# Seven block products for three down projections of the first feed-forward, with partial sums and the residual stream in HBM, and a tail without GpSimd

## The chip, the cores and the metric

The kernel runs on one core of a Trainium2 chip. A core has five engines that work beside each other: TensorE (PE, matrix products; PEld is its weight loading), VectorE (DVE), ScalarE (ACT), GpSimd (POOL) and SyncE (SP, which here only starts DMAs). Each executes its own list of instructions in order and waits on semaphores. The metric is the device time of one launch in microseconds. Before the change the median is 879.47 us of three runs, from 879.43 to 879.74. All data are fp32.

## The reference, cut to what matters

One layer of a decoder on x of 512 tokens by 1024 channels: a half-step feed-forward, a mixer, a second half-step feed-forward, each with an RMS norm ahead of it and another behind it.

```
def swiglu(x, w_gu, w_down):
    gate, up = jnp.split(x @ w_gu, 2, axis=-1)
    return (jax.nn.silu(gate) * up) @ w_down
...
x = x + 0.5 * rms_norm(swiglu(rms_norm(x, ffn1_pre_g[l]), ffn1_w_gu[l], ffn1_w_down[l]), ffn1_post_g[l])
y = hybrid_mixer(rms_norm(x, mix_pre_g[l]), ...)
x = x + rms_norm(y, mix_post_g[l])
x = x + 0.5 * rms_norm(swiglu(rms_norm(x, ffn2_pre_g[l]), ffn2_w_gu[l], ffn2_w_down[l]), ffn2_post_g[l])
```

The hidden width is 2816, which is 22 chunks of 128. `w_gu` is 1024 by 5632 and `w_down` 2816 by 1024. The change concerns the down product (the last `@ w_down`) of the first feed-forward and the last norm, the last line, for the last 128 tokens.

## The kernel before, in words

*Precision.* An fp32 product is made of three products of rounded halves: a weight or an activation is split into a high part (a cast on ACT) and a low part (a subtraction on DVE), and PE computes hi·hi, hi·lo and lo·hi (`mm3`, L403 to L408).

*Weights.* The class `Weights` (L50) streams all weights through five raw buffers of 1 MB (`NRAW`). A raw buffer holds several units; for each unit, `cast` makes the high part and `low` the low part. `take` hands the next unit to PE and first makes the units up to four ahead (`AHEAD`). When the last unit of a raw buffer is split, `load` (L69) starts the next raw load on SP. `later` (L100) defers further loads until so many units are taken. Order of work on each engine is the order in which the program writes it, so a cast that stands behind a waiting copy on ACT waits with it.

*First feed-forward.* Activations lie with channels on partitions and 512 tokens along the free dimension. `GROUPS1` cuts the 22 hidden chunks in five groups of 4, 4, 4, 4 and 6. Each group first makes gate and up for its chunks. From chunk 4 on (`CLASSIC1`) this is done two chunks at a time by a Strassen-like scheme of seven block products (`quad`, inner function `seven`, L765 to L772, matmuls 128x256). Then comes the group's part of the down product (the loop at L1076): eight columns c of 128 output channels, each a product of 4 chunks in 3 passes, 12 matmuls 128x512, 96 for the group (18 each and 144 for the last group, of which the last `LATE` = 3 columns are done later). Columns 0 and 1 run interleaved (L1095). Group 0's results are copied by ACT to eight SBUF tiles (L1105), groups 1 to 3 are added by DVE (L1107), and the last group goes to `res.chunk` (L566), which adds the partial sum and squares it for the norm behind. The residual stream xT stays in two raw buffers all along (`stream`, L470), so the weights have three.

*Side work.* In group 2, at c == 2, `decay_factor` (L1008) computes constants of the recurrence with some 20 small DVE operations and one exponential; a table load for Silu follows. In the last group GpSimd loads and prepares gates and masks of the mixer.

*Second feed-forward.* Here tokens are on partitions in the result. `GROUPS2` has groups of 6, 4, 4, 4 and 4 chunks. The three middle ones (`SEVEN_DOWN`) take the down product by `seven_down`: the block of 512 hidden channels by 1024 outputs is cut in two along both sides, the tokens in two halves, and seven block products replace eight, 12 matmuls 128x512 each, 84 for the group. The hidden forms (sums of blocks) come out of the quads, the weight forms are combined in place in the raw buffers by DVE (`combine`, L305 and its neighbours; casts at L294). A finished pair of PSUM banks is copied to a stage tile by ACT (L1556), and GpSimd starts an accumulating DMA that adds the stage tile to partial sums in HBM (L1558); the last form goes to two places. Group 0 stored its parts plainly (L1590), the second half of the outputs negated. The residual stream is lent to HBM meanwhile (L1592), so the weights have five raw buffers, and given back ahead of the last group (L1602), as are the parts (L1598).

*Tail.* The last group goes by blocks of 128 tokens (L1618 to L1666). Per piece, DVE adds the partial sum (L1642), ACT squares and sums (L1643), GpSimd multiplies by the gain (L1649); then the sum of squares, a root on ACT (L1656), a reciprocal on DVE (L1657), and one DVE operation that scales and adds the residual (L1665), and an output DMA (L1666). For the last 128 tokens (`end`) there are three pieces, of 512, 256 and 256 channels: piece 2 is multiplied by DVE into a tile of its own (L1647), and piece 1 is scaled by ACT (L1662) and added by GpSimd to a copy `tail` that ACT made of the residual (L1638, L1663).

Of the kernel before, what the change touches and what calls it, by code (L numbers as in the profile page):

```python
# [32 lines left out]
CLASSIC1, CLASSIC2 = 4, 6  # L33
SEVEN_DOWN = 6, 18
PUMPS = [(2, 1)] * 8 + [(1, 1), (1, 0), (4, 0)]
# [14 lines left out]
class Weights:  # L50
# [3 lines left out]
    def __init__(self):  # L54
        self.raws, self.tiles, self.left, self.units = [], {}, [], []
        self.loaded = self.rounded = self.split = self.taken = 0
        self.ready, self.todo = {}, []

# [27 lines left out]
    def fill(self, n, early=False):  # L86

        while self.split < min(self.taken + n, len(self.units)):
            if self.rounded == self.split:
                self.round()  # L90
            raw, _, low, _ = self.units[self.split]
            low(self.tiles[raw], *self.ready[self.split])
            self.split += 1
            self.left[raw] -= 1
            if not self.left[raw]:
                self.load()
            if early and self.rounded == self.split:
                self.round()
# [18 lines left out]
def tile_layer(ctx: ExitStack, tc: tile.TileContext, out: bass.AP, **ins: bass.AP):  # L117
# [84 lines left out]
    def add_quad(w_gu, f, name):  # L202
# [32 lines left out]
        unit(b, "v")  # L235

# [43 lines left out]

    def add_seven_down(f):

        wd = ins["ffn2_w_down"]
        rx, ry = (W.raw(lambda i=i: load_raw([wd[0, (f + k) * P:(f + k + 2) * P, HALF_D[i]] for k in (0, 2)], 2, D, f"b{'yx'[i]}d{f}_")) for i in (1, 0))
        first, second = HALF_D
        b11, b21, b12, b22 = (ry, first), (ry, second), (rx, first), (rx, second)

        def of(block):
            return W.tiles[block[0]][:, :, block[1]]

        def unit(block, n, pre=None):
            def cast(raw):
                hi, lo = w_tiles(2, T, f"bd{n}{f}_")
                act.copy(hi, of(block))  # L294
                return hi, lo

            def low(raw, hi, lo):
                dve.tensor_sub(lo, of(block), hi.bitcast(F32))

            W.unit(block[0], cast, low, pre)  # L300

        def combine(fn, o, x, y):
            def run():
                assert max(o[0], x[0], y[0]) < W.loaded
                fn(of(o), of(x), of(y))  # L305
            return run


        unit(b11, "p", combine(dve.tensor_add, b12, b12, b22))
        unit(b12, "q")  # L310
        unit(b21, "r", combine(dve.tensor_add, b12, b12, b11))
        unit(b12, "s", combine(dve.tensor_sub, b11, b12, b22))
        unit(b22, "t", combine(dve.tensor_add, b21, b12, b21))
        unit(b21, "u")
        unit(b11, "v")

    for f0, f1 in GROUPS2:
        for f in range(f0, f1, 2):
            (add_gate_up if f < CLASSIC2 else add_quad)(w2, f, "b")
        if SEVEN_DOWN[0] <= f0 < SEVEN_DOWN[1]:  # L320
            add_seven_down(f0)
# [233 lines left out]
    class Residual:  # L555
# [24 lines left out]
        def late(self, c, ps, part, h):  # L580
            sl = HALF[h]
            if part is not None:
                self.ys[c] = part
                dve.tensor_add(part[:, sl], ps[:, sl], part[:, sl])
            else:
# [103 lines left out]
    class Hidden:  # L689
# [166 lines left out]
        def seven_forms(self, f):  # L856
# [4 lines left out]
            return self.forms  # L861


    n1 = Next("a", gain=lambda c: g1[:, c:c + 1])
# [207 lines left out]
    hid = Hidden("a", n1)  # L1072
    res = Residual("r1", lambda c: half_g[:, c:c + 1])
    parts = [None] * KD
    late = []
    for g, (f0, f1) in enumerate(GROUPS1):  # L1076
        xs = hid.chunks(f0, f1) if g else hid.classic(f1, banks, {})
        if f1 == FC:
            preload(AF.Sqrt)
        for c in range(KD):  # L1080
            if f1 == FC and c == 0:
                load_gates()
                neg = masks()
            if f1 == FC and c == 3:
                split_gates()
            if g == 2 and c == 2:
                ka, nka = decay_factor()
                preload(AF.Silu)
            if f1 == FC and c >= KD - LATE:
# [448 lines left out]

    def seven_down(f):
        forms = hid.seven_forms(f)  # L1540
        A, B, Dd, E_ = ([bank(f"y{s}{f}{i}") for i in range(2)] for s in "abde")

        def seven(banks, form, first, stop):
            w = hi, lo = W.take()
            hh, hl_ = forms[form]
            for i in range(2):
                for k in range(2):
                    js = slice(k * (T // 2) + i * P, k * (T // 2) + (i + 1) * P)
                    pe.matmul(banks[i], hh[:, js], hi[:, k, :], start=first and k == 0, stop=False, skip_group_check=True)  # L1549
                    pe.matmul(banks[i], hh[:, js], lo[:, k, :], start=False, stop=False, skip_group_check=True)  # L1550
                    pe.matmul(banks[i], hl_[:, js], hi[:, k, :], start=False, stop=k == 1, skip_group_check=True)  # L1551

        def to_parts(banks, *blocks):
            for i in range(2):
                st = t2k("stage")
                act.copy(st, banks[i])  # L1556
                for tb, dh in blocks:
                    pool.dma_start(parts[2 * tb + i, dh], st, accum_op=ALU.add)  # L1558

        for banks, form, blocks in ((A, "a11", []), (Dd, "s3", [(1, 1)]), (B, "a12", [(0, 0)]), (A, "s2", [(1, 0)]),  # L1560
                                    (E_, "s4", [(0, 1)]), (Dd, "a22", [(1, 0)]), (A, "s1", [(1, 1), (0, 1)])):
            seven(banks, form, form in ("a11", "s3", "s4"), True)
            if hid.steps:
                hid.steps.pop(0)()
            if form == "a11":
                for i in range(2):
                    act.copy(B[i], A[i])
            else:
                to_parts(banks, *blocks)

    for g, (f0, f1) in enumerate(GROUPS2[:-1]):
        if g:
            if g == 1:
                W.later(4, W.load, 2)
            seven_down(f0)
# [15 lines left out]
        for x, h in zip(x_tiles, xT_hbm):  # L1591
            pool.dma_start(h, x)  # L1592
    f0, f1 = GROUPS2[-1]
# [5 lines left out]
    hs = hid.chunks(f0, f1, ahead=5)  # L1599
    x_tiles, xT[:] = stream()  # L1600
    for x, h in zip(x_tiles, xT_hbm):
        pool.dma_start(x, h)  # L1602
    preload(AF.Sqrt)
# [14 lines left out]
    for tb in range(NB):  # L1618
# [8 lines left out]
        for i, f in steps:  # L1627
            dh, c0, c1 = pieces[i]
            if (i, f) == (1, f1 - 1 if tb == 0 else f0):

                tp = []
                for h in range(2):
                    tp.append(bank(f"otp{tb}{h}"))
                    for c in range(4):
                        pe.transpose(tp[h][:, c * P:(c + 1) * P], xT[4 * h + c][:, tb * P:(tb + 1) * P], ident)
                if end:
                    tail = wt("tail")[:, :T // 2]
                    act.copy(tail, tp[1][:, :T // 2])  # L1638
            mm3_out(banks[i][:, :c1 - c0], hs[f - f0], tb, weights(f, dh), f % 2, slice(c0, c1), f == f0, f == f1 - 1)
            if f == f1 - 1:  # L1640
# [3 lines left out]
                if end and i == 2:  # L1644
                    dve.tensor_add(tot, ss[:, 0:1], ss[:, 1:2])
                    last = wt("last")[:, :c1 - c0]
                    dve.tensor_mul(last, y, grow[dh][:, c0:c1])  # L1647
                else:
                    pool.tensor_mul(y, y, grow[dh][:, c0:c1])  # L1649
        if end:  # L1650
# [7 lines left out]
        for i, (dh, c0, c1) in enumerate(pieces):  # L1658
            y = parts[tb, dh][:, c0:c1]
            if end and i == 1:  # L1660

                act.activation(y, y, AF.Copy, scale=rs)  # L1662
                pool.tensor_add(y, y, tail)  # L1663
            else:
                dve.scalar_tensor_tensor(y, last if end and i == 2 else y, rs, tp[dh][:, c0:c1], op0=ALU.mult, op1=ALU.add)  # L1665
            (act if end and i == 1 else sync).dma_start(out[0, tb * P:(tb + 1) * P, dh * T + c0:dh * T + c1], y)  # L1666
# [28 lines left out]
```

## Time and profile before

| what | us |
|---|---|
| median of three runs (lowest, highest) | 879.47 (879.43, 879.74) |
| the profiled execution, its own time | 880.96 |
| its span; granted clock 0.994 | 879.2 |
| PE busy | 866.2 |
| DVE, ACT, POOL busy | 680.0, 491.3, 176.0 |
| down product of groups 1, 2, 3, first feed-forward | 21.79 each |
| gate and up of a group of four chunks | 40.31 |
| down product of the three middle groups, second feed-forward | 19.07 each |

The profile is of one execution. Its span is measured from the first to the last instruction; what lies around it makes the execution's own time. Engines' busy times overlap. A row of groups gives the line of the kernel, engine, operation, output and input tiles with their shapes, then count and durations. A DMA has two durations: that of its issue on the queue's engine, and that until it has landed. The tiles `ya` are PSUM results of the first feed-forward's down product, `yp_a` its partial sums, `yb` and `yp_b` the same of the second, `ybl` the results of the second's last group, `stage` the tiles on the way to HBM, `otp` the residual stream turned to tokens.

### The profile page before, as it was taken

The page shows a single profiled execution, that of the slowest core. Times are in us where ns is not written, and L with a number is a line of the kernel's source. Part 1 is how long each engine was busy: PE and PEld are TensorE (multiplying, and loading weights), DVE is VectorE, ACT ScalarE, POOL GpSimd, SP SyncE. Part 2 cuts the span into 40 slices and gives each one's busy share as a digit, 9 for nine tenths or more (in the row PEclk, how much of TensorE's full clock was granted, in tenths as well). Part 3 has the DMA queues.
Part 4 walks back from the last instruction along what each step waited for, and adds up shares of the span by engine and source line. Part 5 has one row for each costly group of instructions (what it writes and reads, how often), then busy time and mean ns, then how long its engine had stood idle before and what let it go on. Part 6 is the DMA issues. An engine that isn't in the chain of part 4 may idle for free.

```text
span 879.2 us, 14431 instructions
## 1 busy us (share of the span) xinstructions
PE 866.2 (99%) x5732; PEld 795.2 (90%) x5732; DVE 680.0 (77%) x982; ACT 491.3 (56%) x839; POOL 176.0 (20%) x179
## 2 busy tenths in 40 slices
PE   9999999999999999999999999999999999999995
PEld 8988999989989998998787899888998998998995
DVE  4979758768678864889999589678788789888744
ACT  6647534544435554466787456445556657567542
POOL 2010000000000014444465055211102303205213
PEclk9999999999999999999999999999999999999998
DMA  7242343242243243321311140226573947839901
GB/s 241 74 148 84 103 127 114 73 133 84 73 143 97 84 148 116 97 84 62 109 36 48 49 144 2 96 74 201 188 255 104 229 125 166 196 97 243 279 26 73
DMA packets 91556, 106.10 MB, mean 121 GB/s; under 512 B 4752, under 2 KB 76768, under 8 KB 90976
## 3 DMA queue, kind: packets, MB, share of 16 engines
q1 hardware_dynamic: 83408, 85.64, 30.8%
q0 software_dynamic: 7936, 19.41, 9.5%
q8 instruction: 45, 0.74, 0.3%
q14 instruction: 23, 0.19, 0.1%
q10 hardware_dynamic: 144, 0.13, 0.0%
HBM read 87.86 MB, written 17.30 MB: 120 GB/s over the span
## 4 chain that ended last, share of the span: by engine, by line
PE 91%; DVE 5%; ACT 1%; issue 1%; DMA 1%; POOL 0%; SPq 0%; POOLq 0%; DVEq 0%; ACTq 0%
PE aa L772 12%; PE ab L772 10%; PE da L772 6%; PE db L772 5%; PE ya L408 4%; PE ya L406 4%; PE ya L407 4%; PE ba L772 3%; PE bb L772 3%; PE a_first L948 2%; PE yb L1533 1%; PE yb L1532 1%; PE yb L1534 1%; PE ya L1549 1%; PE ya L1550 1%; PE ya L1551 1%
## 5 line engine op out<-in xcount | busy, mean ns | idle before, releaser
L1558 POOL DMA_DIRECT2D yp_b<-stage x42 | 36.5, 1146 | 147.2 <-ACT stage L1556 138.1
L406 PE MATMUL ya<-hha,whi_ad 128*128 128x512 f32 x158 | 61.5, 389 | 0.0
L407 PE MATMUL ya<-hla,whi_ad 128*128 128x512 f32 x158 | 61.5, 389 | 0.0
L408 PE MATMUL ya<-hha,wlo_ad 128*128 128x512 f32 x158 | 61.5, 389 | 0.0
L1049 POOL MEMSET bd_w_rg<- 128x512 f32 x1 | 0.5, 527 | 266.0 <-PE aa L772 266.0
L408 PEld LDWEIGHTS ya<-hha,wlo_ad 128*128 128x128 f32 x158 | 29.7, 188 | 6.2
L407 PEld LDWEIGHTS ya<-hla,whi_ad 128*128 128x128 f32 x158 | 29.7, 188 | 6.1
L406 PEld LDWEIGHTS ya<-hha,whi_ad 128*128 128x128 f32 x158 | 29.7, 188 | 6.0
L1107 DVE TENSOR_TENSOR yp_a<-ya,yp_a 128x512 f32<-128x512 f32 x24 | 16.4, 686 | 8.8 <-PE ya L408 8.8
L1532 PE MATMUL yb<-whi_bd,hhb 128*128 128x512 f32 x48 | 18.7, 389 | 0.0
L1533 PE MATMUL yb<-wlo_bd,hhb 128*128 128x512 f32 x48 | 18.7, 389 | 0.0
L1534 PE MATMUL yb<-whi_bd,hlb 128*128 128x512 f32 x48 | 18.7, 389 | 0.0
L578 POOL TENSOR_TENSOR acca_r<-acca_r,sq_r 128x512 f32<-128x512 f32 x6 | 8.4, 1406 | 48.1 <-ACT sq_r L437 48.1
L183 DVE TENSOR_TENSOR wlo_bd<-raw_bd,whi_bd 128x1024 fp32r<-128x1024 f32 x10 | 12.1, 1222 | 7.0 <-ACT whi_bd L178 7.0
L1649 POOL TENSOR_TENSOR yp_b<-yp_b,grow 128x512 f32<-128x512 f32 (+1 forms) x8 | 9.7, 1219 | 32.7 <-ACT ysq L1643 32.7
L425 PE MATMUL an<-xh_mx,whi_xl 128*128 128x256 f32 x64 | 15.9, 289 | 0.0
L426 PE MATMUL an<-xh_mx,wlo_xl 128*128 128x256 f32 x64 | 15.5, 283 | 0.0
L705 POOL TENSOR_TENSOR usb<-usb,gsb 128x512 f32<-128x512 f32 x5 | 7.6, 1537 | 33.0 <-DVE usb L702 21.8
L406 PE MATMUL gt<-xh_mx,whi_gt 128*128 128x512 f32 x32 | 14.2, 443 | 0.0
L1643 ACT ACTIVATE ysq<-yp_b 128x512 f32<-128x512 f32 (+1 forms) x9 | 5.2, 583 | 15.1 <-DVE yp_b L1642 14.6
L1532 PE MATMUL ybl<-whi_bd,hhb 128*128 128x512 f32 (+1 forms) x36 | 13.5, 375 | 0.0
L1533 PE MATMUL ybl<-wlo_bd,hhb 128*128 128x512 f32 (+1 forms) x36 | 13.2, 366 | 0.0
(1726 smaller groups left out, 3654.8 us busy)
## 6 DMA issues: line engine op xcount, KB each, us to landing
yp_b<-stage POOLq DMA_DIRECT2D x50, 256.0 KB, 8.2
raw_bd<-in_ffn_w_down SPq DMA_DIRECT2D x4, 1024.0 KB, 8.0
xn<-in_x SPq DMA_DIRECT2D x8, 256.0 KB, 5.2
raw_q<-in_w_in SPq DMA_DIRECT2D x4, 512.0 KB, 3.7
xT_hbm<-xT POOLq DMA_DIRECT2D x2, 1024.0 KB, 11.4
yp_b<-yp_b POOLq DMA_DIRECT2D x8, 256.0 KB, 4.3
xT<-xT_hbm POOLq DMA_DIRECT2D x2, 1024.0 KB, 8.1
out_dram<-yp_b SPq DMA_DIRECT2D x7, 256.0 KB, 2.9
```

What stands on the lines that cost most here:

```text
L406: pe.matmul(ps, hi[:, k, :], xh, start=start, stop=False)
L407: pe.matmul(ps, hi[:, k, :], xl, start=False, stop=False)
L408: pe.matmul(ps, lo[:, k, :], xh, start=False, stop=stop)
L425: pe.matmul(ps[:, sl], hi[:, k, :], xh, start=k == 0, stop=False)
L426: pe.matmul(ps[:, sl], lo[:, k, :], xh, start=False, stop=False)
L772: pe.matmul(o, w[:, k, js], x, start=first and i + j + k == 0, stop=k == 3 and i == 2, skip_group_check=True)
L948: pe.matmul(banks[j][:, HALF[0]], ws[j][part][:, k, :], n1.xs[k][xpart][:, HALF[0]], start=k == 0 and part == xpart, stop=stop and k == KD ...
L1107: dve.tensor_add(parts[c], b, parts[c])
L1532: pe.matmul(ps, hh[:, blk], hi[:, k, cs], start=start, stop=False)
L1533: pe.matmul(ps, hh[:, blk], lo[:, k, cs], start=False, stop=False)
L1534: pe.matmul(ps, hl_[:, blk], hi[:, k, cs], start=False, stop=stop)
L1558: pool.dma_start(parts[2 * tb + i, dh], st, accum_op=ALU.add)
```

## The change

1. *Down products of groups 1 to 3 of the first feed-forward.* The column products are replaced by seven block products. `seven_down` and the weight side `add_seven_down` become functions for both feed-forwards; what differs is how one block product is issued: `by_tokens` as before, and the new `by_channels`, where weights stand in PE and hidden forms of 256 tokens move, 24 matmuls 128x256 for a block, 168 for a group. Per group the weights come in two loads of 1 MB (each of two DMAs) instead of four of 512 KB, with 7 units of 128x1024 and four combinations by DVE.
2. *Partial sums in HBM.* Group 0's eight columns go through stage tiles to HBM, the second half of the channels negated; the blocks of groups 1 to 3 are added there by 14 accumulating DMAs per group; in the last group eight DMAs bring the parts back, and `chunk` and `late` subtract for the channels of the second half. The DVE additions of L1107 go.
3. *Residual stream in HBM.* It is lent after column 4 of group 0 and given back in the last group: `owed` puts the return in the place of the next two raw loads. In between two more raw loads are under way.
4. *Decay factors* move from group 2 to the last group, and the table load for Silu there goes.
5. *Tail.* For the last 128 tokens DVE makes all three multiplications, in place, and all three final steps; ACT's copy and scaling and GpSimd's addition go. The output DMA of piece 1 stays on ACT's queue.

```diff
-SEVEN_DOWN = 6, 18
+SEVEN_DOWN1, SEVEN_DOWN2 = (4, 16), (6, 18)
...
             if not self.left[raw]:
-                self.load()
+                if self.owed:
+                    self.owed.pop(0)()
+                else:
+                    self.load()
...
+        if SEVEN_DOWN1[0] <= f0 < SEVEN_DOWN1[1]:
+            add_seven_down(ins["ffn1_w_down"], f0, "a")
+            continue
...
             if part is not None:
-                dve.tensor_add(part, ps, part)
+                (dve.tensor_sub if c >= KD // 2 else dve.tensor_add)(part, ps, part)
...
+    def seven_down(hid, f, one, part):
+        forms = hid.seven_forms(f)
+        A, B, Dd, E_ = ([bank(f"y{s}{hid.name}{f}{i}") for i in range(2)] for s in "abde")
+        for banks, form, blocks in ((A, "a11", []), (Dd, "s3", [(1, 1)]), (B, "a12", [(0, 0)]), (A, "s2", [(1, 0)]),
+                                    (E_, "s4", [(0, 1)]), (Dd, "a22", [(1, 0)]), (A, "s1", [(1, 1), (0, 1)])):
+            one(banks, W.take(), forms[form], form in ("a11", "s3", "s4"))
+            if hid.steps:
+                hid.steps.pop(0)()
+            for i in range(2):
+                if form == "a11":
+                    act.copy(B[i], A[i])
+                    continue
+                st = t2k("stage")
+                act.copy(st, banks[i])
+                for half, dh in blocks:
+                    o = part(half, dh, i)
+                    pool.dma_start(o, st.rearrange("p (a b) -> p a b", a=2) if len(o.shape) == 3 else st, accum_op=ALU.add)
...
+    in_hbm = [hbm.tile([P, 2, 2, T // 2], F32, name=f"yp_a{i}") for i in range(KD // 2)]
...
+    def by_channels(banks, w, h, first):
+        (hi, lo), (hh, hl_) = w, h
+        for m in range(4):
+            o, ms = banks[m // 2][:, HALF[m % 2]], slice(m * P, (m + 1) * P)
+            for k in range(2):
+                js = HALF[k]
+                for i, (a, x) in enumerate(((hi, hh), (hi, hl_), (lo, hh))):
+                    pe.matmul(o, a[:, k, ms], x[:, js], start=first and i + k + m % 2 == 0, stop=k == 1 and i == 2, skip_group_check=True)
+
+    def lend(tiles):
+        for x, h in zip(tiles, xT_hbm):
+            pool.dma_start(h, x)
+
+    def give_back():
+        tiles, xT[:] = stream()
+        for x, h in zip(tiles, xT_hbm):
+            pool.dma_start(x, h)
+        return tiles
...
     for g, (f0, f1) in enumerate(GROUPS1):
+        if SEVEN_DOWN1[0] <= f0 < SEVEN_DOWN1[1]:
+            if g == 1:
+                W.later(4, W.load, 2)
+            seven_down(hid, f0, by_channels, lambda half, dh, i: in_hbm[2 * dh + i][:, half])
+            continue
+        if f1 == FC:
+            W.owed = [lambda: None, lambda: x_tiles.__setitem__(slice(None), give_back())]
         xs = hid.chunks(f0, f1) if g else hid.classic(f1, banks, {})
         if f1 == FC:
-            preload(AF.Sqrt)
+            for c in range(KD):
+                parts[c] = t2k(f"yp_a{c}")
+                pool.dma_start(in_halves(parts[c]), in_hbm[c // 2][:, :, c % 2])
         for c in range(KD):
...
+            if f1 == FC and c == 1:
+                ka, nka = decay_factor()
+                preload(AF.Sqrt)
...
-            if g == 2 and c == 2:
-                ka, nka = decay_factor()
-                preload(AF.Silu)
...
             if g == 0:
-                parts[c] = t2k(f"yp_a{c}")
-                act.copy(parts[c], b)
-            elif f1 < FC:
-                dve.tensor_add(parts[c], b, parts[c])
+                st = t2k("stage")
+                act.activation(st, b, AF.Copy, scale=-1.0 if c >= KD // 2 else 1.0)
+                pool.dma_start(in_hbm[c // 2][:, :, c % 2], in_halves(st))
+                if c == 4:
+                    lend(x_tiles)
...
-                if end:
-                    tail = wt("tail")[:, :T // 2]
-                    act.copy(tail, tp[1][:, :T // 2])
...
                 if end and i == 2:
                     dve.tensor_add(tot, ss[:, 0:1], ss[:, 1:2])
-                    last = wt("last")[:, :c1 - c0]
-                    dve.tensor_mul(last, y, grow[dh][:, c0:c1])
-                else:
-                    pool.tensor_mul(y, y, grow[dh][:, c0:c1])
+                (dve if end else pool).tensor_mul(y, y, grow[dh][:, c0:c1])
...
-            if end and i == 1:
-                act.activation(y, y, AF.Copy, scale=rs)
-                pool.tensor_add(y, y, tail)
-            else:
-                dve.scalar_tensor_tensor(y, last if end and i == 2 else y, rs, tp[dh][:, c0:c1], op0=ALU.mult, op1=ALU.add)
+            dve.scalar_tensor_tensor(y, y, rs, tp[dh][:, c0:c1], op0=ALU.mult, op1=ALU.add)
```

More of the change, by code (lines that the diff above doesn't have):

```diff
@@ L235, in add_quad, with add_seven_down, of, unit @@
         unit(b, "v")
+    def add_seven_down(wd, f, name):
+        rx, ry = (W.raw(lambda i=i: load_raw([wd[0, (f + k) * P:(f + k + 2) * P, HALF_D[i]] for k in (0, 2)], 2, D, f"{name}{'yx'[i]}d{f}_")) for i in (1, 0))
+        first, second = HALF_D
+        b11, b21, b12, b22 = (ry, first), (ry, second), (rx, first), (rx, second)
+        def of(block):
+            return W.tiles[block[0]][:, :, block[1]]
+        def unit(block, n, pre=None):
+            def cast(raw):
+                hi, lo = w_tiles(2, T, f"{name}d{n}{f}_")
+                act.copy(hi, of(block))
+                return hi, lo
+            def low(raw, hi, lo):
+                dve.tensor_sub(lo, of(block), hi.bitcast(F32))
+            W.unit(block[0], cast, low, pre)
+        def combine(fn, o, x, y):
+            def run():
+                assert max(o[0], x[0], y[0]) < W.loaded
+                fn(of(o), of(x), of(y))
+            return run
+        unit(b11, "p", combine(dve.tensor_add, b12, b12, b22))
+        unit(b12, "q")
+        unit(b21, "r", combine(dve.tensor_add, b12, b12, b11))
+        unit(b12, "s", combine(dve.tensor_sub, b11, b12, b22))
+        unit(b22, "t", combine(dve.tensor_add, b21, b12, b21))
+        unit(b21, "u")
+        unit(b11, "v")
     for add in add_pair([w1[0, :, o + P:o + 2 * P] for o in (0, F)], KD, "second", (dve, pool)):
@@ L279, in add_down @@
             add_unit(r, lambda raw, i=i: raw[:, i:i + 2, :], 2, T, f"bd{f + i}{dh}")
[L281 to L315, printed above, removed]
     for f0, f1 in GROUPS2:
@@ L1537, in tile_layer, with by_tokens @@
     parts = {(tb, dh): hbm.tile([P, T], F32, name=f"yp_b{tb}{dh}") for tb in range(NB) for dh in range(2)}
[L1539 to L1567, printed above, removed]
-            else:
-                to_parts(banks, *blocks)
+    def by_tokens(banks, w, h, first):
+        (hi, lo), (hh, hl_) = w, h
+        for i in range(2):
+            for k in range(2):
+                js = slice(k * (T // 2) + i * P, k * (T // 2) + (i + 1) * P)
+                pe.matmul(banks[i], hh[:, js], hi[:, k, :], start=first and k == 0, stop=False, skip_group_check=True)
+                pe.matmul(banks[i], hh[:, js], lo[:, k, :], start=False, stop=False, skip_group_check=True)
+                pe.matmul(banks[i], hl_[:, js], hi[:, k, :], start=False, stop=k == 1, skip_group_check=True)
     for g, (f0, f1) in enumerate(GROUPS2[:-1]):
@@ L1590, in tile_layer @@
                 pool.dma_start(parts[tb, dh], st)
-        for x, h in zip(x_tiles, xT_hbm):
-            pool.dma_start(h, x)
+        lend(x_tiles)
     f0, f1 = GROUPS2[-1]
@@ L1599, in tile_layer @@
     hs = hid.chunks(f0, f1, ahead=5)
[L1600 to L1602 removed]
+    give_back()
     preload(AF.Sqrt)
```

13 lines of the change are left out of this document (7 added, 6 removed).

## The prediction

> **What bounds the kernel now.** I read four views, in this order. First the profile's page: the span, the busy times and the chain that ended last.
>
> ```profile
> span 879.2 us, 14431 instructions
> PE 866.2 (99%) x5732; PEld 795.2 (90%) x5732; DVE 680.0 (77%) x982; ACT 491.3 (56%) x839; POOL 176.0 (20%) x179
> PE 91%; DVE 5%; ACT 1%; issue 1%; DMA 1%; POOL 0%; SPq 0%; POOLq 0%; DVEq 0%; ACTq 0%
> ```
>
> The reader is to see that PE works through 99% of the span and carries 91% of the chain. So PE time counts one for one, and what DVE, ACT, POOL and the DMAs do counts only where PE would wait for it or where PE is done. In the list of waits PE has six rows, 3.6 us together, none of them in a down product.
>
> Second, the table of busy time by stretches. Row 1 is the first of the three down products to be changed, row 2 the gate and up of the next group; rows 3 and 4 are the same two things in the second feed-forward, whose three middle groups are by seven block products already. Columns: stretch, length, busy PE, PEld, DVE, ACT, POOL, granted clock, DMA share, GB/s.
>
> ```profile
> 120.38:142.17 21.79, 21.79 (x99) 18.03 (x98) 15.53 (x21) 7.73 (x11) 0.00 (x0) 1.00 0.46 145
> 142.17:182.48 40.31, 40.31 (x338) 40.31 (x337) 28.59 (x34) 20.34 (x32) 0.00 (x0) 1.00 0.24 79
> 666.38:685.45 19.07, 19.07 (x87) 15.77 (x86) 17.06 (x20) 14.49 (x23) 6.88 (x8) 1.00 0.69 165
> 685.45:725.76 40.31, 40.31 (x338) 40.31 (x337) 33.62 (x34) 24.06 (x32) 5.28 (x7) 1.00 0.70 171
> ```
>
> PE is busy for the whole of every row. A down product by columns is 96 matmuls 128x512 in 21.79 us, 227 ns each; by seven blocks of tokens it is 84 in 19.07 us, again 227 ns. Gate and up are 336 matmuls 128x256 in 40.31 us, 120 ns each, every one with its own weight load. The rows end up to two matmuls over.
>
> Third, the accumulating DMA of the second feed-forward, by its line: issue on GpSimd, then landing.
>
> ```profile
> L1558 POOL DMA_DIRECT2D yp_b<-stage x42: 846/1182/2047, 674.8 to 810.2; - x42
> ...
> DMA to landing us min/median/max: 4.6/8.7/13.4
> ```
>
> Fourth, the tail in order of time, and the line on which all engines meet at the end.
>
> ```profile
> 867.24 0.68 DVE L1642 TENSOR_TENSOR yp_b<-ybl,yp_b 128x512 f32<-128x512 f32 x1
> 870.06 0.42 DVE L1642 TENSOR_TENSOR yp_b<-ybl,yp_b 128x256 f32<-128x256 f32 x1 [1.01 <-PE ybl L1534]
> 872.57 0.47 DVE L1665 SCALAR_TENSOR_TENSOR yp_b<-last,rs_b,otp 128x256 f32<-128x256 f32 x1
> ...
> 868.75 1.98 POOL L1649 TENSOR_TENSOR yp_b<-yp_b,grow 128x512 f32<-128x512 f32 x2 [2.29 <-ACT ysq L1643]
> 872.48 0.73 POOL L1663 TENSOR_TENSOR yp_b<-yp_b,tail 128x256 f32<-128x256 f32 x1 [1.74 <-ACT yp_b L1662]
> ...
> L1691 POOLq DRAIN x3: 51/93/5991, 872.4 to 878.9; - x3
> L1691 SPq DRAIN x3: 7/7/7, 875.6 to 878.7; - x3
> ```
>
> SP has all its output landed at 875.6, yet GpSimd's drain of 5.99 us, begun at 872.44 around the addition at 872.48, ends at 878.4; 0.76 us later the span is over. GpSimd's drain ends last.
>
> **The change part by part.**
>
> *PE, three groups.* 96 matmuls 128x512 go (21.79 us), 168 of 128x256 come (weights stand still, 256 tokens move). The new shape's price is the gate and up row: 40.31/336 = 120 ns. So 168 x 0.120 = 20.16, which is 1.63 less per group and **4.9 us less** in three. Columns fall by an eighth, but two prices (227 for 512, 120 for 256) give 13 ns per matmul besides its columns, and 72 more matmuls give 0.94 back of the 2.57 saved. The row's own bounds: 40.31/338 is 119.3 ns, thus 5.25 in all. If each block cost what the token form does, 19.07, it would be 2.72 x 3 = 8.2; the shape is not that, so I take it as no end.
>
> The Trainium skill, "TensorE: Matmul & The Clock Gate", section "Back-to-back issue gap", lists 262 cycles at 256 columns and 518 at 512, by which, at the 2.4 GHz of the warm clock on that page, I estimate 21.8 - 18.3 = 2.4 saved per group of its (faster) pace, 7.1 in three. The trace disagrees: 227 and 120 ns at a granted clock of 1.00, so the larger fixed part stands and the sum keeps 4.9.
>
> *DVE and ACT beside it.* 24 additions L1107 of 686 ns leave DVE. Per group 8 halves of 128x512 become 7 of 128x1024 and 4 combinations; 12 copies to stage tiles and 2 bank copies go to ACT, 14 accumulating DMAs to GpSimd. This is the second feed-forward's list instruction for instruction: 17.06 + 33.62 = 50.7 us DVE and 38.6 ACT in 59.38. Here there are 20.16 + 40.31 = 60.47 for it. PE covers it, cost 0; if the cover is gone, PE waits for a weight block at W.take.
>
> *Stage tiles and banks.* A block's ACT copy into a stage tile waits until an earlier accumulation has landed, three products before: 8.16 us in the second feed-forward, 3 x 2.88 = 8.64 here. Behind that copy ACT has weight casts queued, and for them PE waits. There, with landings of 8.7 median and 13.4 at worst, ACT's waits name no DMA, and PE has no wait; here the time is 6% longer. Cost 0; at the other end, (13.4 - 8.64) = 4.8 per group.
>
> *GpSimd and SP in the first feed-forward.* GpSimd is idle for 266 us before L1049. It gets 8 stores (540 ns each at L1590), 2 lends, 42 accumulations at 1.18 (50 us), 8 loads of parts, 2 returns. The loads wait for the last accumulation, at most to the end of the last group's gate and up; residual r1 needs them only then plus the first column pair, two of 18 matmuls at 227 ns, 8.2 us. The landing of such a load is 4.3. Masks and gates, queued behind, start where they started. SP has 6 fewer loads. The first group's raw slot is later by the lend (11.4 to landing, slot free by some 88 instead of 85), and PE needs that unit at about 106: hidden.
>
> *The small chain of decay factors* (some 20 small DVE operations, +2.05 us, the difference of the stretch 182.48 to 204.27 to its sisters) moves into the last group, where DVE is busy for 9.9 of 20.5 us. Cost 0; one table load goes, also hidden.
>
> *Tail.* GpSimd's two multiplications (1.98) and addition (0.73), ACT's copy (0.35) and scaling (0.51) leave; DVE gets multiplications of 0.69 and 0.41 and a final step of 0.39. Each multiplication is in place, so it waits for ACT's square of the same piece, and later DVE work queues behind. In this span's clock: square of piece 0 read out 868.67, multiplication to 869.38; difference of piece 1 (until now 868.62 to 869.04) to 869.80; square, then multiplication to 870.88; difference of piece 2 to 871.30 (870.48 before); square to 872.0, multiplication to 872.43; sum, root, reciprocal to 873.37; the three final steps to 874.98. They ended at 873.04. So DVE is **1.94 later**, and the last output lands near 877.5 instead of 875.6. But GpSimd's last work is now at 866.5, before; if its 6 us drain starts there, it is over by 872.5, and the end is SP's 877.5 + 0.76 = 878.3: **0.9 less** than 879.2. Bounds: DVE's serial order costs nothing and the end is 875.6 + 0.76, -2.8; or a drain of the same length still ends last, moved with DVE, +1.9. I take -0.9: both parts are read from the tail's rows.
>
> *Sum:* -4.9 - 0.9 = -5.8. The profiled execution took 880.96 (span 879.2), 1.49 above the median 879.47 of the runs shown; the difference is carried. Span 873.4, profiled execution 875.2, median **873.7 us**.
>
> **The rivals.**
>
> A. The tail loses: GpSimd's drain, or what it stands for, is a closing cost that follows the last engine, not its own addition. The tail then gives +1.9: 879.5 - 4.9 + 1.9 = 876.5. For it: 5.99 us is far longer than the addition. Against: it began with the addition, where DVE's drain (1.12 us) covers just DVE's last work.
>
> B. DVE's waits on the squares are shorter than written and the drain goes: 871.8, with 119.3 ns 871.4. Against: three in-place pieces on one queue.
>
> C. Slower. Accumulations land later than a stage tile is wanted: ACT stands, weight casts come late, PE waits. At 4.8 us per group, 14.3 in all: 879.5 - 5.8 + 14.3 = 888.0. It decides from 1.9 us per group (5.8/3). For it: 13.4 at worst is beyond 8.64, and 1 KB rows in stores and loads. Against: the second feed-forward, same tiles and DMA share 0.69, with PE 19.07 of 19.07. In "SBUF — State Buffer", section "SBUF: two separate sides", the Trainium skill warns that GpSimd cannot write descriptors while DVE holds the shared port; the trace has that lengthening at most (issues of 846 to 2047 ns against 540 for plain stores), and no wait of PE from it.
>
> D. The new shape does not pay, the change doing nothing for PE: from 21.79/168 = 129.7 ns per matmul on; then 879.5 - 0.9 = 878.6. Against: 120 ns for 338 in a row, with the same weight tiles' columns and one load per matmul.
>
> **How the numbers follow.** Forecast with its neighbourhood 0.53, A 0.14, B 0.13, C 0.08, D 0.04; a small PE wait at the seams, costing 1 to 4 us (875 to 878), 0.08. The range 871.4 to 876.6 runs from B to A and leaves out C, D and half of the seams, 0.16. A measurement here tells 0.2%, 1.76 us, from no change: faster is below 877.7. Faster: 0.53 + 0.14 + 0.13 + 0.07 = 0.87. Same: D and the last of the seams, 0.05. Slower: C, 0.08.
>
> **What would show it.** The three new products in 20.1 to 20.2 us each with PE busy throughout (wrong from 21.79); no PE row in the list of waits for a weight tile of the first feed-forward; gate and up still at 40.31; ACT's stage copies without a DMA as releaser; residual r1's additions without a wait for the parts; the decay chain beside PE. In the tail, DVE's last step 1.5 to 2 us later against PE's last matmul, and GpSimd's long drain over before SP's last landing. The prediction is wrong if PE stands in the first feed-forward or the long drain comes back at the end.

## The result, and the profile after

The changed kernel takes 873.5 us (873.44 to 873.61, four runs) beside 879.51 for the kernel before: a ratio of 0.9929, 95% interval 0.9916 to 0.9942. That is 6.0 us less, where 5.8 were forecast. The total was right; two of its terms were not, and that they nearly cancel is luck. First the page of the changed kernel's profile.

```profile
PE 859.9 (99%) x5948; PEld 800.2 (92%) x5948; DVE 702.8 (81%) x979; ACT 520.8 (60%) x871; POOL 223.3 (26%) x238
DVE 0%; ACT 0%; issue 0%; DVEq 0%
```

PE still fills 99% of the span of 871.8 us. The chain has lost its way back to PE at a step that the trace calls "issue", so here it tells only of the last 9 us. The profiled execution took 873.51 us.

Now the table of stretches: the new products of group 1, the gate and up behind them, the new products of group 3 (columns as before).

```profile
118.95:139.11 20.16, 20.16 (x170) 20.16 (x169) 18.17 (x20) 15.43 (x24) 7.06 (x8) 1.00 0.69 164
139.11:179.43 40.32, 40.32 (x338) 40.32 (x337) 32.53 (x34) 23.20 (x31) 5.27 (x6) 1.00 0.69 167
239.91:260.07 20.16, 20.16 (x170) 20.16 (x169) 18.16 (x20) 15.40 (x24) 7.06 (x9) 1.00 0.71 133
```

20.16 us, PE busy throughout, at the price of 120 ns per matmul. The second group's stretch, not shown, is 20.16 us as well. Next, the accumulating DMA of the first feed-forward by its line; its landings are given together with those of the second feed-forward, which now has the same line:

```profile
L886 POOL DMA_DIRECT2D yp_a<-stage x42: 851/1192/2072, 127.5 to 265.2; - x42
...
DMA to landing us min/median/max: 4.5/8.6/13.6
```

These are nearly the durations of the second feed-forward before the change (846/1182/2047 and 4.6/8.7/13.4). Last, the changed tail in order of time: the last matmul, two of DVE's multiplications with the difference between them, and its final steps; then the line on which the engines meet.

```profile
864.36 0.28 PE L1596 MATMUL ybl<-whi_bd,hlb 128*128 128x256 f32 x1
...
864.98 0.43 DVE L1680 TENSOR_TENSOR yp_b<-yp_b,grow 128x256 f32<-128x256 f32 x1 [0.62 <-ACT ysq L1677]
865.32 0.42 DVE L1676 TENSOR_TENSOR yp_b<-ybl,yp_b 128x256 f32<-128x256 f32 x1
...
866.38 0.43 DVE L1680 TENSOR_TENSOR yp_b<-yp_b,grow 128x256 f32<-128x256 f32 x1 [0.57 <-ACT ysq L1677]
...
867.43 1.53 DVE L1691 SCALAR_TENSOR_TENSOR yp_b<-yp_b,rs_b,otp 128x512 f32<-128x512 f32 x3
```

```profile
L1717 POOLq DRAIN  x3: 51/98/3048, 859.8 to 871.5; - x3
L1717 SPq DRAIN  x3: 7/7/7, 871.0 to 871.3; - x3
```

The drain is an instruction near the end of each engine's list; DVE's, 1.57 us from 867.5, covers just its last steps. DVE waits for ACT's squares, and the difference of the last piece (865.32) stands behind such a wait. The last step ends at 868.96, and SP has its output landed at 871.0. GpSimd's drain, 3.05 us from 859.8, is long over.

To compare kernels I cut each span at two PE events that the change leaves alone: the first matmul of group 0's down product, and the start of the last matmul. What lies ahead of the first is called the start, what lies between them the middle, the rest the closing.

| us | start | middle | closing | span |
|---|---|---|---|---|
| before | 58.15 | 811.59 | 9.46 | 879.2 |
| changed | 56.88 | 807.48 | 7.44 | 871.8 |
| difference | -1.27 | -4.11 | -2.02 | -7.4 |

The difference in the start is mostly not the change's. The clock that TensorE was granted differs there from execution to execution; the table of stretches, from 10 to 15 us, before and then changed:

```profile
10.00:15.00 5.00, 5.00 (x35) 5.00 (x34) 4.62 (x10) 4.11 (x9) 2.30 (x2) 0.77 1.08 330
```

```profile
10.00:15.00 5.00, 5.00 (x44) 5.00 (x44) 5.00 (x12) 4.11 (x9) 2.08 (x2) 1.00 1.10 363
```

35 against 44 matmuls, at a clock of 0.77 against 1.00. That is most of the 1.49 us by which the profiled execution of before lay above its median. Without it the spans differ by 6.13, as the medians do (6.0). Over all profiles below, the start runs from 56.45 to 59.99, so I judge by middle and closing, and give the medians beside them.

### The profile page after: what moved, and what is told of

Same layout as the page of the kernel before. It is cut to its first block, busy times and chain, and to the rows that moved or that the text cites. A ratio compares the mean times of both kernels' runs of the same rounds, so it can differ in the third digit from the quotient of the medians.

```text
span 871.8 us, 15066 instructions
## 1 busy us (share of the span) xinstructions
PE 859.9 (99%) x5948; PEld 800.2 (92%) x5948; DVE 702.8 (81%) x979; ACT 520.8 (60%) x871; POOL 223.3 (26%) x238
## 3 DMA queue, kind: packets, MB, share of 16 engines
q0 software_dynamic: 15840, 38.81, 19.6%
## 5 line engine op out<-in xcount | busy, mean ns | idle before, releaser
L886 POOL DMA_DIRECT2D yp_a<-stage x42 | 36.8, 1137 | 146.9 <-ACT stage L883 136.8
L886 POOL DMA_DIRECT2D yp_b<-stage x42 | 36.3, 1110 | 148.3 <-ACT stage L883 139.6
L412 PE MATMUL ya<-hla,whi_ad 128*128 128x512 f32 x62 | 24.2, 390 | 0.0
L411 PE MATMUL ya<-hha,whi_ad 128*128 128x512 f32 x62 | 24.1, 389 | 0.0
L413 PE MATMUL ya<-hha,wlo_ad 128*128 128x512 f32 x62 | 24.1, 389 | 0.0
L186 DVE TENSOR_TENSOR wlo_bd<-raw_bd,whi_bd 128x1024 fp32r<-128x1024 f32 x10 | 12.1, 1223 | 7.0 <-ACT whi_bd L181 7.0
L710 POOL TENSOR_TENSOR usb<-usb,gsb 128x512 f32<-128x512 f32 x5 | 7.6, 1535 | 33.0 <-DVE usb L707 21.8
L1680 POOL TENSOR_TENSOR yp_b<-yp_b,grow 128x512 f32<-128x512 f32 x6 | 7.7, 1289 | 29.6 <-ACT ysq L1677 29.6
L1140 POOL DMA_DIRECT2D yp_a<-yp_a x8 | 6.4, 890 | 32.2 <-PE aa L777 25.8
L413 PEld LDWEIGHTS ya<-hha,wlo_ad 128*128 128x128 f32 x62 | 11.6, 188 | 2.4
L412 PEld LDWEIGHTS ya<-hla,whi_ad 128*128 128x128 f32 x62 | 11.6, 188 | 2.4
L411 PEld LDWEIGHTS ya<-hha,whi_ad 128*128 128x128 f32 x62 | 11.6, 188 | 2.4
L1630 POOL DMA_DIRECT2D yp_b<-stage x8 | 4.4, 549 | 36.0 <-ACT stage L1629 35.6
```

Source lines behind the costliest of these rows:

```text
L186: low.tensor_sub(two(lo, x), x, two(hi.bitcast(F32), x))
L411: pe.matmul(ps, hi[:, k, :], xh, start=start, stop=False)
L412: pe.matmul(ps, hi[:, k, :], xl, start=False, stop=False)
L413: pe.matmul(ps, lo[:, k, :], xh, start=False, stop=stop)
L886: pool.dma_start(o, st.rearrange("p (a b) -> p a b", a=2) if len(o.shape) == 3 else st, accum_op=ALU.add)
L1680: (dve if end else pool).tensor_mul(y, y, grow[dh][:, c0:c1])
```

## The experiments

Two questions were open: why the middle gave 4.1 where the products alone gave 3 x (21.79 - 20.16) = 4.9, and why the closing gave 2.0 where I had 0.9. The theory at first: a loss of 0.8 at the seam to the mixer by the moved decay factors, and a tail that is worth 2.0 by itself.

**1. The products without the new tail.**

```diff
...
-                (dve if end else pool).tensor_mul(y, y, grow[dh][:, c0:c1])
+                if end and i == 2:
...
+                    dve.tensor_mul(last, y, grow[dh][:, c0:c1])
+                else:
+                    pool.tensor_mul(y, y, grow[dh][:, c0:c1])
...
+            if end and i == 1:
+                act.activation(y, y, AF.Copy, scale=rs)
+                pool.tensor_add(y, y, tail)
...
```

> The changed kernel with the tail of before. Theory: first feed-forward and tail are separate gains. From the first down product to the last matmul the changed kernel's profile is 4.1 us shorter, of that 4.9 by the three products and 0.8 lost again at the seam to the mixer. So 879.5 - 4.1 = 875.4, GpSimd's last drain near 6 us again. Rival (the prediction's sum: the products give 4.9 and nothing is lost): 874.6.

Measured: 872.88 us (872.4 to 874.2) beside 879.69, ratio 0.9923 (0.9911 to 0.9935). The middle is 807.43, as in the changed kernel. But the closing is 6.74, not 9.46: the old tail, behind the new products, is shorter than the new one. The line on which the engines meet:

```profile
L1728 POOLq DRAIN  x3: 51/98/2478, 867.0 to 870.7; - x3
L1728 SPq DRAIN  x3: 7/7/7, 870.1 to 870.4; - x3
```

The same drain, behind the same addition of 0.72 us, takes 2.48 us instead of 5.99, and SP's landing ends the kernel. Theory (875.4) and rival (874.6) both missed this.

**2. The new tail without the products.** The edit of `end` in the diff of the change, alone, on the kernel before.

> The kernel before with the tail of the changed one. Theory: the whole 2.0 us that the changed profile is shorter from the last matmul on belong to the tail: 879.5 - 2.0 = 877.5, GpSimd's drain over before SP's last landing. Rival (the prediction's term, with part of the difference being one odd execution of before): 879.5 - 0.9 = 878.6.

Measured: 878.41 us (877.0 to 880.8) beside 879.69, ratio 0.9987 (0.9978 to 0.9996). In its profile the closing is 7.46, the start 59.99. So the closing is 2.0 shorter, as the theory said; the median shows 1.3 of it and lies nearer the rival's 878.6, under a start that scatters by more than that.

```profile
L1680 POOLq DRAIN  x3: 51/98/6556, 867.0 to 878.8; - x3
L1680 SPq DRAIN  x3: 7/7/7, 878.3 to 878.6; - x3
```

Here the drain is 6.56 us, 3.5 longer than behind the same tail in the changed kernel, but it begins at 867.0 and is hidden. So the new tail gains 2.0 where the drain is long and costs 7.44 - 6.74 = 0.7 where it is short; in the changed kernel it is short.

**3. The decay factors alone**, moved to the last group in the kernel before.

```diff
-        if f1 == FC:
-            preload(AF.Sqrt)
...
-            if g == 2 and c == 2:
+            if f1 == FC and c == 1:
                 ka, nka = decay_factor()
-                preload(AF.Silu)
+                preload(AF.Sqrt)
```

> The kernel before with only the decay factors moved to the last group. Theory: their chain of 5.1 us on DVE, with a wait for ACT's exponential, delays residual r1's second column; GpSimd's additions of squares then come late and lie beside DVE's low part of the mixer's weights, which gets 0.8 longer: 880.3, and that low part 2.3 us instead of 1.55. Rival (the seam's 0.8 comes from the loads of the parts or the stream's return): 879.5.

Measured: 881.08 us (880.33 to 882.54) beside 879.69, ratio 1.0015 (1.0006 to 1.0023). The middle grows by 0.81, from 811.59 to 812.40, and the low part is 2.32 us: there the theory holds. The median grows by 1.4, against 0.8 forecast; the closing is as before, so by the profile the rest lies in the start and is no part of the theory.

**4. The decay factors one step earlier** in the changed kernel: `c == 1` becomes `c == 0`.

> The changed kernel with the decay factors one step earlier, ahead of the last group's first two columns, where DVE and ACT stood idle for 2.9 and 4.5 us. Theory: the second column is no longer late, the collision goes: 873.5 - 0.8 = 872.7, the low part back at 1.55 us. Rival: 873.5.

Measured: 872.84 us (872.66 to 874.54), ratio 0.9924 (0.9912 to 0.9935); the middle is 806.77, 0.71 less. The mechanism can be read in three places. DVE in the changed kernel, residual r1's first and second column with the decay chain between them (its first operation and the one behind its wait for ACT are shown), then the mixer's low part:

```profile
328.26 0.69 DVE L573 TENSOR_TENSOR yp_a<-ya,yp_a 128x512 f32<-128x512 f32 x1 [2.88 <-PE ya L413]
328.87 0.16 DVE L1041 TENSOR_SCALAR nabs<-cols 128x4 f32<-128x4 f32 x1
...
331.17 0.17 DVE L1046 TENSOR_SCALAR s<-z 128x4 f32<-128x4 f32 x1 [1.94 <-ACT z L1044]
...
333.92 0.69 DVE L573 TENSOR_TENSOR yp_a<-ya,yp_a 128x512 f32<-128x512 f32 x1
...
343.51 2.33 DVE L186 TENSOR_TENSOR wlo_xl<-raw_xl__4061,whi_xl 128x1024 fp32r<-128x1024 f32 x1 [1.64 <-ACT whi_xl L181]
```

GpSimd in the changed kernel; DVE's low part with the earlier decay factors; and, in the kernel before, the two columns in one, GpSimd's last addition and the low part:

```profile
342.09 2.67 POOL L583 TENSOR_TENSOR acca_r<-acca_r,sq_r 128x512 f32<-128x512 f32 x2
```

```profile
343.33 1.55 DVE L186 TENSOR_TENSOR wlo_xl<-raw_xl__4061,whi_xl 128x1024 fp32r<-128x1024 f32 x1 [1.64 <-ACT whi_xl L181]
```

```profile
334.39 1.37 DVE L568 TENSOR_TENSOR yp_a<-ya,yp_a 128x512 f32<-128x512 f32 x2 [2.21 <-PE ya L408]
...
348.81 1.30 POOL L578 TENSOR_TENSOR acca_r<-acca_r,sq_r 128x512 f32<-128x512 f32 x1 [2.13 <-ACT sq_r L437]
...
349.63 1.55 DVE L183 TENSOR_TENSOR wlo_xl<-raw_xl__3686,whi_xl 128x1024 fp32r<-128x1024 f32 x1 [1.63 <-ACT whi_xl L178]
```

The second column, which followed the first directly in the kernel before, ends at 334.6 because the chain lies between. ACT's square and GpSimd's sum follow late, and GpSimd's last two additions (to 344.76) cover 1.25 us of DVE's low part (343.51 to 344.76), where in the kernel before one covered 0.48 (349.63 to 350.11). From the end of GpSimd's addition to its own end the low part takes 1.08 us in the one kernel and 1.07 in the other. So it takes 0.78 us longer, and everything behind it on DVE is later: the late columns, their sums of squares, and PE's `rms_r`, which waits 1.3 us instead of 0.5 (0.5 again with the edit). The Trainium skill, "SBUF — State Buffer", section "SBUF: two separate sides", calls the port pair of DVE and GpSimd an exclusive lock, which a DVE operation with two SBUF inputs meets; the rows agree, 2.33 and 1.55 us here for an operation whose like in L186 takes 1.22 elsewhere.

**5. and 6. What makes the drain short?** An instruction fetch in the tail was the first theory. I moved the boundaries of GpSimd's instructions without adding DMAs.

```diff
+    pad = const.tile([P, 1], F32, name="pad")
     for g, (f0, f1) in enumerate(GROUPS1):
+        if g == 1:
+            for _ in range(60):
+                pool.memset(pad, 0.0)
```

> The kernel before with 60 small memsets on GpSimd in its idle time ahead of group 1, which give it about as many more instructions as the changed kernel has, and no more DMAs. In the profiles GpSimd's last drain is 3.5 us longer in every kernel without the first feed-forward's seven products, whatever its tail, and an instruction fetch lies in the tail of these and of none of the others. Theory: GpSimd's drain waits for the fetch of a block of instructions that happens to begin at the kernel's end; 60 more instructions move the boundary: drain 2.5 us, from the last matmul to the end 6.7 instead of 9.5, median 879.5 - 2.7 = 876.8. Rival (the drain depends on the DMAs that GpSimd has started, 62 more in the changed kernel): 879.5 and a drain of 6.0.

> The same 60 memsets in the kernel before with the changed tail. Theory: without the long drain the changed tail is 0.7 us slower than the old one (7.4 from the last matmul to the end, against 6.7): 877.5. Rival (the changed tail is worth 2.0 by itself): with the padding 876.8 - 2.0 = 874.8.

Measured: 880.78 (880.02 to 881.19) and 878.93 us (878.1 to 880.43) beside 879.5, ratios 1.0011 (1.0002 to 1.002) and 0.999 (0.9981 to 0.9999). Closings 9.46 and 7.54, the drains what they were, 5.99 and 6.56. The theory of the fetch falls; the rival, the DMAs that GpSimd started, remained. The medians are higher than either theory had them. One cause is in the traces: in the four padded kernels (runs 5 to 8) PE waits 0.64 to 0.70 us at about 23 us, in the start, for ACT's cast `xh_a`, and in no other profile here does it wait there. What in the padding brings this about was not tried.

**7. and 8. The number of GpSimd's DMAs.** The kernel before starts 62 of them (8 stores, 42 accumulations, 8 loads, 2 lends, 2 returns), the changed one 124. One more, a load of the norm's gains at the start of every kernel, is not counted here.

```diff
+    pad = const.tile([P, 16], F32, name="pad")
+    spare = hbm.tile([P, 16 * 62], F32, name="spare")
     for g, (f0, f1) in enumerate(GROUPS1):
+        if g == 1:
+            pool.memset(pad, 0.0)
+            for i in range(62):
+                pool.dma_start(spare[:, 16 * i:16 * (i + 1)], pad)
```

> The kernel before with 62 small DMAs (128 rows of 64 B) that GpSimd starts in its idle time ahead of group 1, into a spare buffer: with its own 62 that makes 124, as many as the changed kernel has. Theory (the length of GpSimd's last drain goes by the DMAs that it has started): the drain is 2.5 us instead of 6.0 and the time from the last matmul to the end 6.7 instead of 9.5, 879.5 - 2.7 = 876.8. Rival (it goes by something else that the seven products change): drain 6.0, 879.5.

> The same with 112 small DMAs, 174 in all, as in the kernel with all parts written twice, where the drain was 7.4 us, 4.3 longer than in the changed kernel with the same tail. Theory: the drain is long again, 2.5 + 4.3 = 6.8 us, and the time from the last matmul to the end near 10.3. Rival: 6.0 as in the kernel before, 9.5.

Measured with 62 more: 877.86 us (877.65 to 878.89) beside 879.71, ratio 0.9974 (0.9965 to 0.9984), closing 6.78. With 112 more: 880.78 (880.3 to 881.24), 1.0006 (0.9997 to 1.0015), closing 9.94. First 62, then 112:

```profile
L1697 POOLq DRAIN  x3: 51/97/3126, 872.1 to 875.9; - x3
```

```profile
L1697 POOLq DRAIN  x3: 51/98/6394, 871.6 to 878.5; - x3
```

62 useless DMAs in GpSimd's idle time shorten the closing by 2.7 us and the kernel by 1.9 (0.7 of the difference is PE's wait in the start), and 50 more lengthen it again. Run 8 alone would decide little, since its 6.39 lies between the theory's 6.8 and the rival's 6.0; the pair decides. So the drain changes with the DMAs that GpSimd has started, neither up nor down steadily. Whether their number is what counts is less sure. By the number the drains with the old tail are long, short, long at 62, 124 and 174. By the packets on GpSimd's queue they are 5.99, 3.13, 6.39 and 2.48 us at 7,936, 9,920, 11,520 and 15,840, up and down once more. The number is thus the simpler reading, not one that excludes the other. The instruction fetches are not it: two lie in the last 14 us here too, with the short drain, and none there in run 9, with a long one.

**9. How near are the landings to setting the pace?** Every store and every accumulation of the first feed-forward's parts is done twice.

```diff
...
                     pool.dma_start(o, st.rearrange("p (a b) -> p a b", a=2) if len(o.shape) == 3 else st, accum_op=ALU.add)
+                    if again:
+                        pool.dma_start(again(half, dh, i), st.rearrange("p (a b) -> p a b", a=2), accum_op=ALU.add)
...
```

> The changed kernel with each store and accumulation of the first feed-forward's parts made a second time into a spare buffer: 100 GpSimd DMAs for 50. Theory (landings are far from setting the pace): PE still does 20.16 and 40.31 us per group, 873.5, at most 0.3 more. Rival C of the prediction (landings are near the reuse of the stage tiles): ACT's stage copies wait, PE with them, from 2 us per group on, 880 or more.

Measured: 885.64 us (884.8 to 886.71), ratio 1.0067 (1.0055 to 1.008). Its middle is 819.14, 11.7 more than in the changed kernel. So the first feed-forward does not bear the double. But it breaks elsewhere than rival C said. Group 3's products in the table of stretches, and the two waits that matter in the last group:

```profile
239.89:260.05 20.16, 20.16 (x170) 20.16 (x169) 18.17 (x20) 15.42 (x24) 10.93 (x13) 1.00 0.87 191
```

```profile
DVE raw_ax__3507 L230 <- DMA raw_ay__3573<-in_ffn_w_gu: 10.5, 1, 10.5
...
PE aa L777 <- ACT u4a L804: 8.8, 1, 8.8
```

The three products keep 20.16. ACT does wait for a landing before two stage copies (3.2 us), without effect on PE. What fails is one load of gate and up weights in the last group, issued at 283.3 as in the changed kernel, used at 292.5 there and at 303.0 here, beside the returning stream and the parts, with the DMA engines busy for 0.93 of the time from 119 to 330 us. GpSimd's queue is late as well: it starts the stream's return at 283.9, in the changed kernel at 265.8. What gives way first is thus the time of the DMAs, not the turn of the stage tiles; whether the DMA engines or GpSimd's queue is the limit, no run here separates.

**10. and 11. Two better kernels.** One is the changed kernel with the old tail and `c == 0`.

> The changed kernel with the tail of before and the decay factors ahead of the last group's first columns. Theory: the two gains over the changed kernel add up, 0.7 at the seam and 0.7 in the tail: 873.5 - 1.4 = 872.1. Rival (one hides the other): 872.8.

Measured: 871.66 us (871.34 to 872.21) beside 879.5, ratio 0.9909 (0.9896 to 0.9923); middle 806.54, closing 6.71. The gains add up. The other has `c == 0` too and keeps DVE's tail, but multiplies into tiles of its own (the list `ym`, empty at first). By run 4, `c == 0` alone leaves the closing at 7.4.

```diff
...
-                if end and i == 2:
-                    dve.tensor_add(tot, ss[:, 0:1], ss[:, 1:2])
-                (dve if end else pool).tensor_mul(y, y, grow[dh][:, c0:c1])
+                if end:
+                    ym.append(wt(f"ym{i}")[:, :c1 - c0])
+                    dve.tensor_mul(ym[i], y, grow[dh][:, c0:c1])
+                    if i == 2:
+                        dve.tensor_add(tot, ss[:, 0:1], ss[:, 1:2])
+                else:
+                    pool.tensor_mul(y, y, grow[dh][:, c0:c1])
...
-            dve.scalar_tensor_tensor(y, y, rs, tp[dh][:, c0:c1], op0=ALU.mult, op1=ALU.add)
+            dve.scalar_tensor_tensor(y, ym[i] if end else y, rs, tp[dh][:, c0:c1], op0=ALU.mult, op1=ALU.add)
```

> The changed kernel with the decay factors ahead of the last group's first columns, and DVE's three multiplications of the last tokens into tiles of their own, so that they need not wait for ACT's squares. Theory (the tail of the changed kernel is longer than the old one because DVE queues behind its waits on the squares): its last step starts 1.0 us earlier after the last matmul, 6.4 from the last matmul to the end instead of 7.4, and 873.5 - 0.7 - 1.0 = 871.8. Rival (the order of the pieces on DVE sets it, not the waits): 7.4 and 872.8.

Measured: 871.48 us (871.15 to 873.11) beside 879.71, ratio 0.9905 (0.989 to 0.9921); closing 6.44.

```profile
863.78 0.42 DVE L1677 TENSOR_TENSOR yp_b<-ybl,yp_b 128x256 f32<-128x256 f32 x1 [0.55 <-PE ybl L1596]
864.24 0.42 DVE L1681 TENSOR_TENSOR ym<-yp_b,grow 128x256 f32<-128x256 f32 x1
```

The last difference now waits for PE alone, and its multiplication follows at once. So it was the in-place multiplication behind ACT's square that cost the changed tail 1.0 us. The edit also puts a small addition of two sums behind the last multiplication; in the changed kernel this addition held ACT's last square back by 0.1 us at most (from 865.74 to 865.84).

**12. The changed kernel beside these.**

> The changed kernel itself beside these. All theories: 873.5, 7.4 us from the last matmul to the end, GpSimd's drain 3.0 us and hidden.

Measured: 873.47 us (873.03 to 874.9), middle 807.49, closing 7.46, drain 3.05. Both better kernels are 1.8 to 2.0 us below it.

## Why the prediction was right, and where not

*PE's products.* 168 x 0.120 = 20.16 per group was forecast and 20.16 measured, 4.9 us in three. The quads' row was the right neighbour for the new shape; the block products of the second feed-forward (19.07) would have promised too much. In the prediction's estimate of 7.1 us in three groups the subtraction is miswritten: 21.8 is the measured time of a group, and the 2.4 is 20.7 - 18.3. The sum does not use it.

*DVE and ACT beside it.* 18.17 + 32.53 = 50.7 us DVE and 38.6 ACT in 60.48 us, the numbers taken over from the second feed-forward. Hidden, as said.

*Stage tiles, landings, parts, lent stream.* No ACT copy waits for a DMA in the first feed-forward, residual r1 never waits for a part, and masks and gates start 6.73 us ahead of the last group's first column in both kernels. Cost 0 holds. Rival C is wrong for this kernel, and in run 9 its mechanism, the reuse of the stage tiles, does not hold PE even with the DMAs doubled.

*The decay factors.* This is a step that failed: "Cost 0", because DVE is busy for 9.9 of 20.5 us. An average over the stretch hid where the chain falls. It holds DVE's queue for 5.1 us, with a wait for ACT inside, between two links of a chain that PE waits for at its end. It cost 0.7 to 0.8 us (0.81 in run 3, 0.71 in run 4).

*The tail.* This is the other step that failed, by its size. The sum read -0.9; the closing shrank by 2.0. Three things were off. First, I laid DVE's durations end to end; neighbours on DVE overlap by some 0.09 us (864.98 + 0.43 is 865.41, the next begins at 865.32), and the last step ends 1.30 us later against the last matmul, not 1.94. Second, I carried the old distance from DVE's end to SP's landing (2.56), but in the old tail the last output goes out behind GpSimd's addition at 873.24; in the new one 2.04 remain. Third, and more important, I gave the vanished drain to GpSimd's earlier end. That works (run 2), but in the changed kernel the drain is short anyway (run 1), and runs 7 and 8 put that down to the DMAs that the other part of the change gives to GpSimd. Seen so, products and DMAs are worth 4.1 + 2.7 = 6.8 us, and the new tail costs 0.7.

*Rivals A and B.* A (the tail loses 1.9 by a drain that comes last) did not occur: the drain starts at GpSimd's last own work, at 859.8. B (DVE's waits on the squares are shorter than written, and the drain goes) is right in part: DVE is 1.30 us later, not 1.94, and the closing's -2.0 lies between the forecast's -0.9 and B's -2.8, a little nearer to B. But the waits are not free; by run 11 they cost 1.0 us. D needed 129.7 ns per matmul; it is 120.

## What to carry to other kernels

Price a new matmul shape by a row of the same shape with the same weight loads in the same kernel; it came out to 0.01 us. A chain of tiny operations that is moved must be followed to its neighbours on the queue, since a stretch that is half idle can still hold the one chain that PE waits for. And before a tail is rearranged to hide a closing cost, see whether that cost still stands once the rest of the change is in: here each part alone removed the same 2 to 3 us.

## What the runs showed of the hardware that was not expected

The length of GpSimd's last drain changes with the DMAs that GpSimd has started in the whole kernel, and not steadily. With the old tail: 62 DMAs, 5.99 us; 124 DMAs, 2.48 (the products) and 3.13 (useless small ones); 174 DMAs, 6.39. With the new tail: 62, 6.56; 124, 3.05; 174, 7.38 (run 9). 60 plain memsets change nothing. Why it changes so, and where it turns, stays open.

TensorE's granted clock is lower soon after the start in some executions and not in others: from 10 to 15 us it was 0.77 in the profile of before, 0.51 in that of run 2 and 1.00 in the changed kernel's, with starts of 58.15, 59.99 and 56.88 us. Other starts differ by up to 1.3 us without it; 0.64 to 0.70 of this is, in the padded kernels, the wait named at runs 5 and 6, and the rest was not tried. Of single microseconds, then, only a comparison of stretches tells.
